# Both parts of h as one moving operand of 512 columns, in an encoder block on one Trainium2 core

## The chip, the cores and the metric

The kernel runs on one core of a Trainium2 chip. The metric is the device time of one execution in microseconds (us), from the first to the last instruction with the little that lies around them. Five engines work at the same time and wait for each other through semaphores: PE (TensorE: matmuls, with weight loads shown apart as PEld), DVE (VectorE), ACT (ScalarE), POOL (GpSimd) and SP (SyncE, which issues most transfers).

## The reference, cut to what matters

`x` is 256 tokens by 2048 channels. One wide projection of the normalised input feeds everything else:

```python
h = rms_norm(x, g_pre)
proj = h @ w_in                      # 256 x 2048 @ 2048 x 10688
mla_in, rwkv_in, z_mla, z_rwkv, gate_mla, gate_rwkv = split(proj)
# attention branch (8 heads) from mla_in; bidirectional recurrent branch (RWKV-7, 16 heads) from rwkv_in
u_mla  = (y_mla  * silu(z_mla))  @ w_br_mla
u_rwkv = (y_rwkv * silu(z_rwkv)) @ w_br_rwkv
out = (sigmoid(gate_mla) * u_mla + sigmoid(gate_rwkv) * u_rwkv) @ w_out
x + rms_norm(out, g_post)
```

## The kernel before

**Two parts.** To keep precision, every float32 operand of a large matmul is split into two float32r parts, hi and lo, with hi + lo the original. A product is then three matmuls: weights hi with h hi, weights hi with h lo, weights lo with h hi. The input h lies in SBUF as `hhi` and `hlo`, channels on partitions, 256 tokens along the row, 16 blocks of 128 channels (`KT`).

**A projection task** (`in_task`, through `cm_task`) makes 256 columns of `proj` as two pieces of 128 output channels. It loads its weights in four chunks of 512 KB (`raw`, three buffers); ACT casts a chunk to `whi` (line 327) and DVE subtracts to get `wlo` (line 330); each has three buffers. For each of the 16 blocks k and each of the two pieces, PE runs lines 396, 397 and 398, all three with 256 moving columns and into the same half of one PSUM bank. So a task uses one bank: piece 0 in its columns 0 to 255, piece 1 in 256 to 511. When the task is done, its `end` stream takes the sums out of the bank (for example `mix` on line 417, `ev_z` on 520, `low_rank_task` on 545).

**Banks.** Eight PSUM banks are named: `d0` to `d2` (pool `DB`, line 215) for projection tasks, `m0` to `m4` (pool `MB`, line 214) for the small products of the two branches.

**The recurrent branch** is worked off in four quads (`Q` 0 to 3, 256 channels each), one after the other. For a quad, `front_d`, `front_k` and `front_v` make its inputs; `chunks_of` then forms the *grams* (line 797 on PE, with the mask multiply on line 191 taking them out of their banks, and transposes on line 805 copied out on line 784), solves a triangular system by 60 small DVE operations and five DVE transposes (lines 818 to 850: the *solve*), and walks through four steps of a recurrence (lines 892 to 944 on PE, 916 to 927 on ACT and DVE). `head_sums` (line 581) are the matmuls of lines 587 and 588.

**Order.** All engines run their instructions in the order in which they were written. That order is made ahead of time by the class `Streams`: each piece of work is a Python generator that asks for an engine with an assumed cost; the class picks the request that can start first, by its own clock, and of those within a small slot the one of the best rank. An operation of a stream is taken as ready `LAG` after the stream's operation before (0.25 us behind PE, 0.12 us behind ACT or DVE, line 49). Projection matmuls have the last rank, so they fill the time that quads leave on PE. `Free.take` hands out banks and work tiles; a stream that finds none waits in the order-making until one is given back. `W.take(KEEP)` asks that more than 6 work tiles are free.

Of the kernel before, what the change touches and what calls it, by code (L numbers as in the profile page):

```python
# [15 lines left out]
S = 256  # L16
D = 2048
# [26 lines left out]
class Streams:  # L44
# [13 lines left out]
    def add(self, gen, rank, t=0.0):  # L58
        s = [gen, rank, t, None]
        self.live.append(s)  # L60
        self._next(s, None)
        return s
# [15 lines left out]
    def run(self, until=None):  # L78
        while self.live and not (until and until()):
# [29 lines left out]
            e, cost = s[3][0], s[3][1]  # L109
            if e == "P":  # L110
# [31 lines left out]
def cD(n):  # L142
    return 0.08 + 1.04e-3 * n
# [11 lines left out]
def encoder_block_kernel(  # L155
# [52 lines left out]
    hhi, hlo = sb([128, KT, S], "hhi", dt=F32R), sb([128, KT, S], "hlo", dt=F32R)  # L208
# [5 lines left out]
    MB = Free(pps.tile([128, 512], F32, tag=f"m{i}", bufs=1, name=f"m{i}") for i in range(5))  # L214
    DB = Free(pps.tile([128, 512], F32, tag=f"d{i}", bufs=1, name=f"d{i}") for i in range(3))
# [155 lines left out]
    def cm_task(src, nk, xhi, xlo, mt, wd, end, kc=4, load_fn=None, ready=None, kready=None, k_first=0,  # L371
                begin=None, pairs=None, first_alone=False):

        parts = []
        nb = (len(mt) + 1) // 2
# [3 lines left out]
        for i, k0 in enumerate(k0s):  # L379
# [23 lines left out]
        def take():  # L403
            b = []
            for _ in range(nb):
                b.append((yield from DB.take()))
            return b

        add_task(parts, begin or take, end, ready)
# [56 lines left out]
    def ev_second(b):  # L466
        yield ("W", lambda: len(have.get("part", ())) == 2)
        for p, m, t, B in zip(b, (96, 128), have["part"], (DB, MB)):
            yield ("D", cD(512))
            tt(w2d(t)[0:m], w2d(t)[0:m], p2(p)[0:m], ALU.add)  # L470
            B.give(p)
# [48 lines left out]
    def ev_z(b, o):  # L520

        z = p2(b[0])
        t = yield from W.take()
        yield ("A", cA(512), None, "exp")
        act.activation(w2d(t), z, AF.Tanh, scale=0.5)
        yield ("D", cD(512))
        stt(o, w2d(t), 1.0, z, ALU.add, ALU.mult)
        W.give(t)
        DB.give(*b)
# [8 lines left out]
    def gate_mla_task(g):  # L538
        def end(b):
            yield ("A", cA(512), None, "exp")  # L540
            act.activation(m16[:, 2 * g:2 * g + 2], p2(b[0]), AF.Tanh, scale=0.5)
            DB.give(*b)
# [1111 lines left out]
```

## Time and profile before

| | us |
|---|---|
| median of three runs | 875.97 |
| lowest and highest | 873.17, 876.22 |
| profiled execution, whole | 872.72 |
| its span, first to last instruction | 870.9 |

The profile is one further execution, 3.25 us below the median and inside 0.5% of it. In it PE is busy for 97% of the span, DVE for 76%, ACT for 58%. PE's matmuls overlap (each is shown with its own full latency), so that neighbouring starts, not the shown length, tell how long one occupies PE.

### The profile page before, as it was taken

The numbers are of one execution on the slowest core, as the hardware profiler recorded it, in microseconds if no ns is written. First come the engines' busy times: TensorE is split into PE (matmuls) and PEld (weight loads), VectorE is DVE, ScalarE is ACT, GpSimd is POOL, SyncE is SP. The second block draws the span as 40 slices with busy tenths as digits, with TensorE's granted clock in tenths as the row PEclk, the third lists the DMA queues.
The fourth block names the chain that finished last, engine by engine and source line by source line (L and its number), as shares of the span: only waits on it lengthen the run. The fifth ranks groups of instructions, "written<-read, shape, count | busy, mean of one in ns | idle before, by whom it ended". The sixth has DMA issues, their size and how long they took to land.

```text
span 870.9 us, 19398 instructions
## 1 busy us (share of the span) xinstructions
PE 848.3 (97%) x8112; PEld 810.0 (93%) x8112; DVE 659.3 (76%) x1082; ACT 501.1 (58%) x797; POOL 30.7 (4%) x66
## 2 busy tenths in 40 slices
PE   9999999999999999999999999999999999999996
PEld 8999999988899998999889999899999999998884
DVE  5878898868987878988789878775867556775554
ACT  6777644487544578354776445586766434444442
POOL 4110000000000000000000000000000000000000
PEclk9999999999999999999999999999999999999999
DMA  9565646633376523565423665346444675555553
GB/s 286 169 181 148 176 129 187 169 99 90 101 212 177 161 68 97 158 193 169 132 76 96 195 188 152 98 149 186 136 128 147 232 257 190 176 193 193 194 195 119
DMA packets 123528, 139.41 MB, mean 160 GB/s; under 512 B 6704, under 2 KB 110512, under 8 KB 123056
## 3 DMA queue, kind: packets, MB, share of 16 engines
q1 hardware_dynamic: 121664, 135.16, 52.4%
q0 software_dynamic: 768, 1.57, 0.6%
q10 hardware_dynamic: 1008, 1.44, 0.5%
q8 instruction: 63, 1.03, 0.5%
q14 instruction: 25, 0.20, 0.1%
HBM read 136.05 MB, written 2.10 MB: 159 GB/s over the span
## 4 chain that ended last, share of the span: by engine, by line
PE 73%; DVE 14%; ACT 8%; issue 2%; DMA 2%; DVEq 0%; ACTq 0%
PE d L396 16%; PE d L398 16%; PE d L397 15%; DVE wlo L330 4%; PE m L1334 2%; PE m L1335 2%; PE m L1336 2%; ACT whi L327 2%; DVE work L191 2%; PE m L398 2%; PE m L396 2%; PE m L397 2%; PE d L1335 1%; PE d L1334 1%; PE d L1336 1%
## 5 line engine op out<-in xcount | busy, mean ns | idle before, releaser
L327 ACT CAST whi<-raw 128x1024 fp32r<-128x1024 f32 (+3 forms) x252 | 252.8, 1004 | 254.2 <-PE d L397 155.1
L330 DVE TENSOR_TENSOR wlo<-raw,whi 128x1024 fp32r<-128x1024 f32 (+3 forms) x250 | 292.4, 1171 | 125.0 <-ACT whi L327 123.4
L396 PE MATMUL d<-hhi,whi 128*128 128x256 f32 (+1 forms) x1296 | 375.1, 289 | 0.0
L398 PE MATMUL d<-hhi,wlo 128*128 128x256 f32 (+1 forms) x1296 | 366.5, 283 | 2.3 <-DVE wlo L330 2.3
L397 PE MATMUL d<-hlo,whi 128*128 128x256 f32 (+1 forms) x1296 | 366.2, 283 | 0.0
L396 PEld LDWEIGHTS d<-hhi,whi 128*128 128x128 f32 (+1 forms) x1296 | 246.8, 190 | 4.5
L398 PEld LDWEIGHTS d<-hhi,wlo 128*128 128x128 f32 (+1 forms) x1296 | 246.9, 190 | 2.7 <-DVE wlo L330 2.7
L397 PEld LDWEIGHTS d<-hlo,whi 128*128 128x128 f32 (+1 forms) x1296 | 247.1, 191 | 0.1
L191 DVE TENSOR_TENSOR work<-work,work 128x512 f32<-128x512 f32 (+5 forms) x64 | 38.8, 612 | 3.9 <-ACT work L575 1.2
L191 DVE TENSOR_TENSOR u<-u,tmp 128x30 f32<-128x30 f32 (+7 forms) x120 | 29.9, 250 | 3.0
L191 DVE TENSOR_TENSOR tmp<-u 128x30 f32<-128x30 f32 (+7 forms) x120 | 29.8, 249 | 2.9
L396 PE MATMUL d<-b,whi 128*128 128x256 f32 x96 | 27.1, 282 | 0.0
L398 PE MATMUL d<-b,wlo 128*128 128x256 f32 x96 | 27.1, 282 | 0.0
L398 PE MATMUL d<-ar,wlo 128*128 128x256 f32 x96 | 27.0, 281 | 0.0
L397 PE MATMUL d<-work,whi 128*128 128x256 f32 x96 | 26.9, 280 | 0.0
L397 PE MATMUL d<-ar,whi 128*128 128x256 f32 x96 | 26.9, 280 | 0.0
L396 PE MATMUL d<-ar,whi 128*128 128x256 f32 x96 | 26.8, 279 | 0.0
L1334 PE MATMUL m<-whi,hhi 128*128 128x512 f32 x60 | 23.3, 389 | 0.0
L1335 PE MATMUL m<-wlo,hhi 128*128 128x512 f32 x60 | 23.3, 389 | 0.0
L1336 PE MATMUL m<-whi,hlo 128*128 128x512 f32 x60 | 23.3, 389 | 0.0
L191 DVE TENSOR_TENSOR g<-m,mask 128x512 f32<-128x512 f32 x32 | 20.6, 686 | 0.0
L797 PE MATMUL m<-ar,u 64*128 64x128 f32 x256 | 19.2, 285 | 0.3 <-DVE g L191 0.3
(334 smaller groups left out, 1487.3 us busy)
## 6 DMA issues: line engine op xcount, KB each, us to landing
raw<-in_w_in_dram SPq DMA_DIRECT2D x160, 512.0 KB, 3.9
raw<-in_w_out_dram SPq DMA_DIRECT2D x32, 512.0 KB, 3.6
raw<-in_w_br_mla_dram SPq DMA_DIRECT2D x16, 512.0 KB, 4.0
raw<-in_w_br_rwkv_dram SPq DMA_DIRECT2D x16, 512.0 KB, 3.3
raw<-in_mla_wkv_b_dram SPq DMA_DIRECT2D x8, 512.0 KB, 3.9
raw<-in_mla_wq_b_dram SPq DMA_DIRECT2D x8, 384.0 KB, 3.3
raw<-in_w_in_dram SPq DMA_DIRECT2D x7, 384.0 KB, 5.3
g<-in_x_dram SPq DMA_DIRECT2D x2, 1024.0 KB, 6.9
```

The lines of the kernel that those rows point to most:

```text
L191: dve.tensor_tensor(out=o, in0=a, in1=b, op=op)
L327: act.copy(dst(c.hi), src(raw))
L330: eng.tensor_tensor(out=dst(c.lo), in0=src(raw), in1=dst(c.hi).bitcast(F32), op=ALU.subtract)
L396: pe.matmul(o, hi[:, c:c + m], xhi(k), start=k == k_first and i % 2 == 0, stop=False)
L397: pe.matmul(o, hi[:, c:c + m], xlo(k), start=False, stop=False)
L398: pe.matmul(o, lo[:, c:c + m], xhi(k), start=False, stop=last)
L797: pe.matmul(m[:, q * 128:q * 128 + 128], z.kb[R64[h], d, j, q], z.ar[d][R64[h], j, q], start=q == 0, stop=q == 3)
L1334: pe.matmul(banks[t], hhi[:, k, T], hi, start=k == 0, stop=False)
L1335: pe.matmul(banks[t], hhi[:, k, T], lo, start=False, stop=False)
L1336: pe.matmul(banks[t], hlo[:, k, T], hi, start=False, stop=k == KT - 1)
```

## The change

Three edits. First, `hhi` and `hlo` become two halves of one tile `hh`, and a projection task runs, per block and piece, one matmul of 512 moving columns (weights hi with h hi and h lo side by side; line 408 of the changed kernel) and one of 256 (weights lo with h hi, added to the first half; line 409). A piece now fills a bank of its own, so a task takes two banks, and its `end` first calls `total`: two ACT copies of the second halves and two DVE adds of the first halves. This goes for 32 tasks; the eight of `gate_rwkv` and the two low-rank tasks at the start keep three matmuls. Second, the pools become four and four banks. Third, `Streams` drops `LAG` where a stream asks twice in a row for the same engine.

```diff
@@ class Streams: add, run
-        s = [gen, rank, t, None]
+        s = [gen, rank, t, None, ""]
...
                     ready = s[2] if len(q) < 3 or q[2] is None else q[2]
+                    if s[4] == q[0] and ready == s[2]:
+
+                        ready -= self.LAG[q[0]]
...
             e, cost = s[3][0], s[3][1]
+            s[4] = e
@@ tiles and banks
-    hhi, hlo = sb([128, KT, S], "hhi", dt=F32R), sb([128, KT, S], "hlo", dt=F32R)
+    hh = sb([128, 2, KT, S], "hh", dt=F32R)
+    hhi, hlo = hh[:, 0], hh[:, 1]
...
-    MB = Free(pps.tile([128, 512], F32, tag=f"m{i}", bufs=1, name=f"m{i}") for i in range(5))
-    DB = Free(pps.tile([128, 512], F32, tag=f"d{i}", bufs=1, name=f"d{i}") for i in range(3))
+    MB = Free(pps.tile([128, 512], F32, tag=f"m{i}", bufs=1, name=f"m{i}") for i in range(4))
+    DB = Free(pps.tile([128, 512], F32, tag=f"d{i}", bufs=1, name=f"d{i}") for i in range(4))
@@ cm_task
+                        if both:
+
+                            o = p2(banks[i])[0:m]
+                            pe.matmul(o, hi[:, c:c + m], both(k), start=k == k_first, stop=False)
+                            pe.matmul(o[:, 0], lo[:, c:c + m], xhi(k), start=False, stop=k == nk - 1)
+                            continue
...
-                steps.append((len(mt) * 3 * 0.119, mm) + (((lambda k=k: kready(k)),) if kready else ()))
+                steps.append((len(mt) * (0.347 if both else 3 * 0.119), mm) + (((lambda k=k: kready(k)),) if kready else ()))
...
-        add_task(parts, begin or take, end, ready)
+        add_task(parts, lambda: take_banks(len(mt) if both else (len(mt) + 1) // 2), end, ready)
@@ in_task and the ends
+        kw.setdefault("both", lambda k: hh[:, :, k])
...
+    def total(b, o):
+
+        for i in range(2):
+            yield ("A", cA(256) - 0.05)
+            act.copy(o[:, i], p2(b[i])[:, 1])
+        for i in range(2):
+            yield ("D", cD(256))
+            tt(o[:, i], p2(b[i])[:, 0], o[:, i], ALU.add)
+            DB.give(b[i])
...
                 t = yield from W.take(KEEP)
-                yield from mix(p2(b[0]), 128, V_MU + 8 * n + 2 * Q, w2d(t))
-                DB.give(*b)
+                yield from total(b, w2d(t))
+                yield from mix(w2d(t), 128, V_MU + 8 * n + 2 * Q, w2d(t))
...
             t = yield from W.take(KEEP)
-            yield ("A", cA(512))
-            act.copy(w2d(t), p2(b[0]))
-            DB.give(*b)
+            yield from total(b, w2d(t))
```

`ev_z` and `gate_mla_task` get `total` in the same way. The order that comes out differs on every engine; three places show how. A name such as `d0_110` is bank `d0` with a serial number.

On PE, a projection task inside a transition between two quads, before: two times three matmuls for block k, pieces 0 and 1, all into bank `d0`.

```order
L396 MATMUL d0_110<-hhi_13_75,whi1_19_81 128x256
L397 MATMUL d0_110<-hlo_14_76,whi1_19_81 128x256
L398 MATMUL d0_110<-hhi_13_75,wlo1_22_84 128x256
L396 MATMUL d0_110<-hhi_13_75,whi1_19_81 128x256
L397 MATMUL d0_110<-hlo_14_76,whi1_19_81 128x256
L398 MATMUL d0_110<-hhi_13_75,wlo1_22_84 128x256
```

And the start of a task in the changed kernel: two matmuls each into `d0` and `d1`, then the next block.

```order
L408 MATMUL d0_108<-hh_13_75,whi1_18_80 128x512
L409 MATMUL d0_108<-hh_13_75,wlo1_21_83 128x256
L408 MATMUL d1_109<-hh_13_75,whi1_18_80 128x512
L409 MATMUL d1_109<-hh_13_75,wlo1_21_83 128x256
L408 MATMUL d0_108<-hh_13_75,whi1_18_80 128x512
L409 MATMUL d0_108<-hh_13_75,wlo1_21_83 128x256
```

What moved: a piece has one matmul fewer, of twice the columns, and a bank of its own.

On PE, the last rows ahead of the grams of quad 3, and the first of these, before (the tile `u8` holds the quad's inputs; between the matmuls of lines 587 and 588 some rows earlier and the grams stand projection matmuls, first into `d0`, then, the task being done, into `d1`):

```order
L398 MATMUL d0_110<-hhi_13_75,wlo0_21_83 128x256
L396 MATMUL d0_110<-hhi_13_75,whi0_18_80 128x256
L397 MATMUL d0_110<-hlo_14_76,whi0_18_80 128x256
L398 MATMUL d0_110<-hhi_13_75,wlo0_21_83 128x256
L396 MATMUL d1_111<-hhi_13_75,whi1_19_81 128x256
L397 MATMUL d1_111<-hlo_14_76,whi1_19_81 128x256
L398 MATMUL d1_111<-hhi_13_75,wlo1_22_84 128x256
L396 MATMUL d1_111<-hhi_13_75,whi1_19_81 128x256
L397 MATMUL d1_111<-hlo_14_76,whi1_19_81 128x256
L398 MATMUL d1_111<-hhi_13_75,wlo1_22_84 128x256
L797 MATMUL m3_108<-ar_182_5302,u8_179_5261 128x128
L797 MATMUL m1_106<-ar_182_5302,u8_179_5261 128x128
```

The same place in the changed kernel, from the last projection matmuls ahead of the grams to the first grams (line 817 is 797 of before, 668 is 648, 607 and 608 are 587 and 588):

```order
L408 MATMUL d2_110<-hh_13_75,whi0_17_79 128x512
L409 MATMUL d2_110<-hh_13_75,wlo0_20_82 128x256
L408 MATMUL d3_111<-hh_13_75,whi0_17_79 128x512
L409 MATMUL d3_111<-hh_13_75,wlo0_20_82 128x256
L668 MATMUL m1_105<-iv_4_66,work7_154_3535 128x128 x2
L668 MATMUL m1_105<-iv_4_66,work17_169_4330 128x128 x2
L607 MATMUL m2_106<-work5_191_4697,bdr_6_68 128x256
L608 MATMUL m2_106<-work8_192_4698,bdr_6_68 128x256
L607 MATMUL m2_106<-work5_191_4697,bdr_6_68 128x256
L608 MATMUL m2_106<-work8_192_4698,bdr_6_68 128x256
L817 MATMUL m3_107<-ar_181_4586,u8_180_4558 128x128
L817 MATMUL m0_104<-ar_181_4586,u8_180_4558 128x128
```

What moved: between line 944 (964 in the changed kernel) and the first gram there were 26 groups of three projection matmuls, and there are now 6 groups of two; the task on `d2` and `d3` ends here, and the next one begins only behind the last gram's transposes, on `d0`.

On DVE, around the same grams, before: the mask multiplies into `g16`, with splits (line 330) and the quad's output work between them.

```order
L191 TENSOR_TENSOR g16_198_5523<-m4_109,mask_1_63 128x512
L191 TENSOR_TENSOR g16_198_5523<-m2_107,mask_1_63 128x512
L194 SCALAR_TENSOR_TENSOR yr_43_113<-yr_43_113,iv_4_66,work12_190_5428 128x256
L330 TENSOR_TENSOR wlo1_22_84<-raw1_16_78,whi1_19_81 128x1024
L191 TENSOR_TENSOR yr_43_113<-yr_43_113,work15_196_5489 128x512
L191 TENSOR_TENSOR g16_198_5523<-m1_106,mask_1_63 128x512
L191 TENSOR_TENSOR g16_198_5523<-m0_105,mask_1_63 128x512
L194 SCALAR_TENSOR_TENSOR yr_43_113<-yr_43_113,iv_4_66,work2_26_88 128x256 x2
```

The same place in the changed kernel: the last four mask multiplies, then the two adds of `total` that set `d0` and `d1` free, then the first split after 22 rows without one.

```order
L195 TENSOR_TENSOR g16_197_4726<-m3_107,mask_1_63 128x512
L195 TENSOR_TENSOR g16_197_4726<-m0_104,mask_1_63 128x512
L195 TENSOR_TENSOR g16_197_4726<-m1_105,mask_1_63 128x512
L195 TENSOR_TENSOR g16_197_4726<-m2_106,mask_1_63 128x512
L195 TENSOR_TENSOR work8_195_4710<-d0_108,work8_195_4710 128x256
L195 TENSOR_TENSOR work8_195_4710<-d1_109,work8_195_4710 128x256
L342 TENSOR_TENSOR wlo0_20_82<-raw0_14_76,whi0_17_79 128x1024
L198 SCALAR_TENSOR_TENSOR yr_42_112<-yr_42_112,iv_4_66,work2_189_4681 128x256 x2
L195 TENSOR_TENSOR yr_42_112<-yr_42_112,work5_194_4709 128x512
```

What moved: the eight mask multiplies stand together, no split is between them, and the banks for the next task come free behind them.

## Rows read from the trace of the kernel before

**Rows 1.** Page: busy time of each engine, share of the span, instructions.

```profile
PE 848.3 (97%) x8112; PEld 810.0 (93%) x8112; DVE 659.3 (76%) x1082; ACT 501.1 (58%) x797; POOL 30.7 (4%) x66
```

**Rows 2.** Busy time by stretch: PE, PEld, DVE, ACT, POOL, granted clock, DMA.

```profile
100.00:560.00 460.00, 449.86 (x5166) 431.43 (x5165) 390.17 (x677) 266.62 (x412) 13.11 (x31) 1.00 0.51 142
```

**Rows 3.** Waits of PE: us in total, times, longest.

```profile
PE m L923 <- DVE work L918: 3.1, 8, 0.7
PE d L398 <- DVE wlo L330: 2.3, 2, 1.2
PE m L587 <- ACT work L435: 1.3, 2, 0.7
```

**Rows 4.** Timeline of PE in a projection task: start, length, instruction.

```profile
682.07 0.28 PE L396 MATMUL d<-hhi,whi 128*128 128x256 f32 x1
...
682.43 0.28 PE L396 MATMUL d<-hhi,whi 128*128 128x256 f32 x1
```

**Rows 5.** Timeline of PE in the output projection, 512 moving columns.

```profile
780.06 0.39 PE L1334 MATMUL d<-whi,hhi 128*128 128x512 f32 x1
...
780.74 0.39 PE L1334 MATMUL d<-whi,hhi 128*128 128x512 f32 x1
```

**Rows 6.** Groups of PE by line: count, busy us, mean ns, idle before.

```profile
L396 PE MATMUL d<-hhi,whi 128*128 128x256 f32 (+1 forms) x1296 | 375.1, 289 | 0.0
...
L396 PE MATMUL m<-hhi,whi 128*128 128x256 f32 x48 | 13.7, 286 | 0.0
```

**Rows 7.** Timeline of PE, a moving operand in two pieces of 128 columns.

```profile
578.19 0.28 PE L1086 MATMUL d<-whi,b 128*128 128x256 f32 x1
578.31 0.28 PE L1087 MATMUL d<-wlo,b 128*128 128x256 f32 x1
```

**Rows 8.** Groups of DVE and ACT that read 256 or 512 columns of PSUM.

```profile
L191 DVE TENSOR_TENSOR work<-m,work 128x256 f32<-128x256 f32 x8 | 3.4, 422 | 3.9 <-PE m L1212 3.9
...
L1205 ACT COPY work<-m 128x256 f32<-128x256 f32 x16 | 5.8, 377 | 1.8 <-PE m L1203 1.8
...
L549 ACT COPY work<-d 128x512 f32<-128x512 f32 x4 | 2.3, 578 | 0.0
```

**Rows 9.** Busy by stretch: quad 0's solve; quad 3's front end; quad 3's grams.

```profile
113.40:173.00 59.60, 59.60 (x498) 59.51 (x497) 51.13 (x95) 27.58 (x32) 0.12 (x1) 1.00 0.59 163
...
448.20:460.50 12.30, 12.27 (x113) 11.85 (x112) 10.83 (x15) 12.15 (x21) 0.52 (x1) 1.00 0.38 103
460.50:472.40 11.90, 11.90 (x124) 11.01 (x124) 11.71 (x20) 7.88 (x13) 0.00 (x0) 1.00 0.27 84
```

**Rows 10.** DVE in quad 0's solve: its one large wait, and the splits.

```profile
DVE wlo L330 <- ACT whi L327: 6.4, 13, 0.7
...
L330 DVE TENSOR_TENSOR wlo<-raw,whi 128x1024 fp32r<-128x1024 f32 x20 | 24.5, 1225 | 6.5 <-ACT whi L327 6.4
```

**Rows 11.** Timeline of ACT ahead of quad 3's grams.

```profile
448.22 1.05 ACT L327 CAST whi<-raw 128x1024 fp32r<-128x1024 f32 x1 [0.33 <-PE d L397]
...
458.96 1.28 ACT L573 ACT_TABLE_LOAD   x1
...
460.80 0.57 ACT L549 COPY work<-d 128x512 f32<-128x512 f32 x1
```

**Rows 12.** Timeline of PE there: recurrence's end, first gram, transposes, second gram.

```profile
448.23 0.69 PE L944 MATMUL m<-g,uv 128*64 128x64 f32 x16
...
460.49 1.16 PE L797 MATMUL m<-ar,u 64*128 64x128 f32 x16
461.58 0.39 PE L396 MATMUL d<-hhi,whi 128*128 128x256 f32 x1
...
462.40 0.60 PE L805 MATMUL m<-iv,u 128*128 128x128 f32 x4
462.76 0.36 PE L396 MATMUL d<-hhi,whi 128*128 128x256 f32 x1
```

**Rows 13.** Timeline of DVE: two grams taken out of their banks.

```profile
461.88 1.28 DVE L191 TENSOR_TENSOR g<-m,mask 128x512 f32<-128x512 f32 x2
```

More of the change, by code (lines that the diff above doesn't have):

```diff
@@ L213, in encoder_block_kernel, with take_banks @@
     W = Free(works[:-1])
-    MB = Free(pps.tile([128, 512], F32, tag=f"m{i}", bufs=1, name=f"m{i}") for i in range(5))
-    DB = Free(pps.tile([128, 512], F32, tag=f"d{i}", bufs=1, name=f"d{i}") for i in range(3))
+    MB = Free(pps.tile([128, 512], F32, tag=f"m{i}", bufs=1, name=f"m{i}") for i in range(4))
+    DB = Free(pps.tile([128, 512], F32, tag=f"d{i}", bufs=1, name=f"d{i}") for i in range(4))
+    def take_banks(n):
+        b = []
+        for _ in range(n):
+            b.append((yield from DB.take()))
+        return b
     yr = sb([128, 8, 256], "yr")
@@ L371, in cm_task @@
     def cm_task(src, nk, xhi, xlo, mt, wd, end, kc=4, load_fn=None, ready=None, kready=None, k_first=0,
-                begin=None, pairs=None, first_alone=False):
+                pairs=None, first_alone=False, both=None):
         parts = []
-        nb = (len(mt) + 1) // 2
         k0s = list(range(k_first, nk, kc))
@@ L467, in ev_second @@
         yield ("W", lambda: len(have.get("part", ())) == 2)
-        for p, m, t, B in zip(b, (96, 128), have["part"], (DB, MB)):
+        for p, m, t in zip(b, (96, 128), have["part"]):
             yield ("D", cD(512))
             tt(w2d(t)[0:m], w2d(t)[0:m], p2(p)[0:m], ALU.add)
-            B.give(p)
+            DB.give(p)
         yield from ev_wd(have["part"][0])
@@ L520, in ev_z @@
     def ev_z(b, o):
-        z = p2(b[0])
+        yield from total(b, o)
         t = yield from W.take()
         yield ("A", cA(512), None, "exp")
-        act.activation(w2d(t), z, AF.Tanh, scale=0.5)
+        act.activation(w2d(t), o, AF.Tanh, scale=0.5)
         yield ("D", cD(512))
-        stt(o, w2d(t), 1.0, z, ALU.add, ALU.mult)
+        stt(o, w2d(t), 1.0, o, ALU.add, ALU.mult)
         W.give(t)
-        DB.give(*b)
     def z_task(c0, key):
@@ L539, in end @@
         def end(b):
+            o = m16[:, 2 * g:2 * g + 2]
+            yield from total(b, o)
             yield ("A", cA(512), None, "exp")
-            act.activation(m16[:, 2 * g:2 * g + 2], p2(b[0]), AF.Tanh, scale=0.5)
-            DB.give(*b)
+            act.activation(o, o, AF.Tanh, scale=0.5)
         in_task(GM0 + 256 * g, end)
@@ L547, in end @@
             t = yield from W.take(KEEP)
-            yield ("A", cA(512))
-            act.copy(w2d(t), p2(b[0]))
-            DB.give(*b)
+            yield from total(b, w2d(t))
             have[key] = t
@@ L1047, in begin @@
             if g == 0:
-                yield ("W", lambda: quads[3].done and len(MB.tiles) > 1)
-                DB.give(MB.tiles.pop())
+                yield ("W", lambda: quads[3].done)
                 att["kT"] = sb([128, 2, 8, 256], "g16", dt=F32R)
@@ L1061, in begin @@
                     tt(t[R64[i]], kr[R64[i]], att["kr"][0][R64[i]].bitcast(F32), ALU.subtract)
-            a = yield from DB.take()
-            b = yield from DB.take()
-            return a, b
+            return (yield from take_banks(2))
         parts = []
@@ L1104, in wq_task @@
         wq_v = wq_b.rearrange("(k p) (h c) -> p k h c", p=128, c=192)
-        def begin():
-            a = yield from DB.take()
-            b = yield from DB.take()
-            return a, b
         parts = []
@@ L1156, in end @@
                 O.add(head(g, i), 1, O.free["D"])
-        add_task(parts, begin, end, lambda: have["qhl"][1] if "qhl" in have else None)
+        add_task(parts, lambda: take_banks(2), end, lambda: have["qhl"][1] if "qhl" in have else None)
     def half_split(src, hi, lo, n):
@@ L1273, in end @@
             th2[g] = t
-        in_task(GR0 + 256 * g, end)
+        in_task(GR0 + 256 * g, end, both=None)
     def split_y():
@@ L1319, in begin @@
                 MB.tiles.clear()
-            a = yield from DB.take()
-            b = yield from DB.take()
-            return a, b
+            return (yield from take_banks(2))
         parts, more = [], []
@@ L1356, in gain @@
             tt(fin["og"][:, t, N], b[t], fin["gpb"][:, N], ALU.mult)
-            DB.give(b[t])
         def end(b):
@@ L1362, in end @@
                 yield from gain(b, t)
+                DB.give(b[t])
             fin["left"] -= 2
@@ L1523, in pairs_first @@
                ("kr", 0 if k0 < 2 else 2 if k0 < 8 else 8))
-    def begin_second():
-        a = yield from DB.take()
-        b = yield from MB.take()
-        return a, b
     LORA = [(0, 96), (128, 96), (256, 128), (384, 128)]
@@ L1532, in encoder_block_kernel @@
     cm_task(None, KT, *HX, LORA, 512, ev_second, kc=2, pairs=pairs_first, load_fn=load_first, kready=lambda k: have.get(("h", k)),
-            k_first=UN, begin=begin_second)
+            k_first=UN)
     rwkv_tasks(0, kready=lambda k: have.get(("h", k)))
```

5 lines of the change are left out of this document (removed).

## The prediction, made before the change was run

> **What bounds the kernel now.** The share of busy time comes first: PE 97% of the span, DVE 76%, ACT 58% [rows 1]. PE's matmuls overlap in the profile, so 97% alone doesn't show that PE is full; the stretches and the waits do. From 100 to 560 us, where the projection tasks fill what the four quads leave, PE is busy for 449.9 of 460 us at a granted clock of 1.00, and DVE for 390.2, which is 85% [rows 2]. Among PE's waits none is above 3.1 us in total [rows 3]: the recurrence's copies (3.1), a split that came late (2.3), the head sums (1.3). So time is won by giving PE less to do, and lost wherever something makes PE wait that now doesn't. DVE, at 85%, is the engine to watch.
>
> **The change, part by part.** *PE's work.* Four neighbouring starts of 256 columns lie 0.36 us apart, 0.120 us for one [rows 4]; three steps of 512 columns take 0.68 us, 0.227 for one [rows 5]. A block and piece costs 3 x 0.120 = 0.360 us before and 0.227 + 0.120 = 0.347 after, 0.013 less. The groups of line 396 count 1296 + 48 = 1344 [rows 6]; the code takes from them 64 of the two low-rank tasks and 256 of the eight `gate_rwkv` tasks, which keep three matmuls. That leaves 1024, and 1024 x 0.013 = 13.3 us. The new moving operand lies in two pieces far apart; line 1086 already moves two pieces of 128 columns and its next start follows after 0.12 us as well [rows 7], so I charge nothing for that.
>
> Here the Trainium skill speaks against the change. By "TensorE: Matmul & The Clock Gate", section "Back-to-back issue gap", a warm matmul costs its columns at 2.4 GHz plus 2.5 ns, so joining two would save 2.5 ns, 2.6 us in all. The rows differ: 256 and 512 columns differ by 107 ns, which is 256 columns at 2.4 GHz, and leave 13 ns fixed in both. The measurement decides; the sum goes on with 13.3.
>
> *The evictions.* Each of 32 tasks gains two ACT copies and two DVE adds of 256 columns out of PSUM. The nearest rows read 0.377 and 0.422 us [rows 8]: 24 us of ACT, less 4 x 0.58 for the low-rank copies that fall away, and 27 us of DVE. Two independent DVE operations overlap by 0.08 us (two grams take 1.28 us, not 2 x 0.68 [rows 13]), so an add holds DVE for 0.34. Neither engine sets the end by itself; what they cost is what PE comes to wait for.
>
> *The solves.* In quad 0's solve PE is full for all of 59.6 us, while DVE works 51.1 [rows 9] and waits 6.4 us, in front of the splits, for ACT's casts [rows 10]; these in turn wait for PE to free a buffer. That wait is the cover. About 20 chunks pass [rows 10]; each is now 8 x 0.013 = 0.10 us shorter on PE, 2.1 in all, and five tasks bring ten adds, 3.4 us. 6.4 - 2.1 - 3.4 = 0.9 us stay, so PE should hardly wait: I take +1 us for the four solves, between 0 and 3.
>
> *The way into quad 3.* This is the largest term against the change. Before, from the recurrence's end (448.23) to the first gram (460.49) is 12.3 us [rows 12], of which ACT is busy for 12.15 [rows 9]: ACT's chain of casts, copies and a table load [rows 11] sets that length, and PE hides it with 26 groups of projection matmuls, 9.4 us. In the changed order 6 groups stand there, 2.1 us, beside 0.7 us of `front_d`'s matmuls that stood ahead of it before; 6.6 us of cover are gone. The reason is in the banks: a low-rank task's `end` waits for a work tile (its copy, line 549, came late before as well, at 460.80 [rows 11]) and holds `d0` and `d1`; before, PE went on in the third bank, now two tasks hold all four. ACT's list there has lost three casts (3.1 us) and gained the second half of `front_d` (about as much), so I keep the 12 us: PE waits 6, between 3 and 9. Behind the grams the next task waits for two mask multiplies and the adds: +1.
>
> *The grams.* Before, projection matmuls stand between the gram matmuls (460.49 to 461.58) and the transposes (462.40 to 462.76) and behind these [rows 12]. DVE empties the two gram banks from 461.88 to 463.16 [rows 13]. In the changed order nine of twelve following groups stand with little or nothing between, and with four `m` banks instead of five the second group needs a bank of the first: PE could begin it 1.6 us after the first one's start, the first bank comes free after 2.1, the other after 2.7. I take 0.5 us each, +4.5 in all; 0 if the spare bank covers it, 9 if DVE has other work first.
>
> *Relief.* In the recurrences one to four k-steps of projection now stand where one or two stood in front of line 923, and same-engine work of a stream runs on without a gap. PE waits there 3.1 us, for the head sums 1.3, and smaller ones [rows 3]; I take -3, between 0 and -6. What follows the last quad, and the start, keep their work: nothing.
>
> **The sum.** -13.3 + 1 + 6 + 1 + 4.5 - 3 = -3.8 us against the profiled execution of 872.72, that is 868.9. The median of the runs lies 3.25 above that execution: 872.2, given as 872. All bounds to one side give -15 or +9.
>
> **The rivals.** *The waits stay hidden.* The dropped `LAG` lets the quads' chains run closer, so banks and operands come early; the gram bank that is spare covers the rest. For it: ACT's three casts fewer on the way into quad 3. Against it: the 6.6 us of cover are gone in any case. The whole change is then -13.3 with at most 5 back, less a little relief: 862 to 868.5.
>
> *The waits take it all.* The way into quad 3 at its upper bound (9) and the grams at 6 to 9: -1 to +4, 875.5 to 880.4.
>
> *Slower: DVE sets the solves.* If the adds don't overlap (0.42 instead of 0.34) and one dependent operation more waits per chunk, the 0.9 us left become a lack; each solve then lasts as long as DVE's list, and 2.5 us in each of four give +10 upon the sum. It decides from the point at which DVE's own work in the stretch exceeds PE's 57.5 us. For it: DVE's 85%. Against it: 6.4 us of measured slack. 880.4 to 888.
>
> *The joined matmul saves almost nothing.* If in this stream a 512-column matmul with a 256-column one behind it took 0.237 us and not 0.227, the saving would be 3 us instead of 13.3 and the sum 10 us worse, 882. Both spacings of the trace speak against that [rows 4, 5]. The page named above would have it so.
>
> **How the numbers follow.** As worked out (868.5 to 875.5) 0.45; hidden 0.25; all taken 0.14; DVE the bound 0.14; no saving 0.02. What a measurement of this kernel tells from no change is about 0.5%, 4.4 us: below 871.6 it is faster, above 880.4 slower. Of the first case about 0.19 lies below 871.6. Faster: 0.25 + 0.19 = 0.44; same: 0.26 + 0.14 = 0.40; slower: 0.14 + 0.02 = 0.16. The range leaves out a sliver of the hidden case and the upper half of the slower ones: 863 to 882. The likeliest case's own is 868.5 to 875.5.
>
> **What the changed profile would show.** PE's term: starts 0.227 and 0.120 us apart inside a task. Solves: PE full, DVE's wait for casts near 1 us instead of 6.4. Way into quad 3: a PE idle of some 6 us ahead of the first gram, ended by DVE's `ar`, with a long run of DVE rows without a split. Grams: PE waits of about half a microsecond ended by DVE `g` or ACT `b`. I would be wrong in the main step if that idle is absent, and in the solves if waits of line 409 for `wlo` add up to more than 3 us.

## The result: 1.2% slower, outside the range

The changed kernel takes 884.89 us, the median of 4 runs (883.29 to 887.56), beside 874.57 us (872.94 to 876.22) for the kernel before in the same job. The ratio is 1.0118, 95% interval 1.0087 to 1.0149. Forecast were 872 us and a range of 863 to 882. Of the runs below, one execution of 1631.8 us (LAG for DVE and ACT) is disturbed and left out of its median.

The profile shows an execution of 887.56 us, with a span of 885.8; before it was 872.72. So the two profiled executions lie 14.8 us apart and the medians 10.3. Line numbers are those of the changed kernel: 408 is the joined matmul, 409 the one with the low part of the weights, 433 the added copy, 817 the grams, 825 their transposes, 943 the recurrence's matmul (797, 805 and 923 before). First the page's busy times (as [rows 1]) and the granted clock in 40 slices:

```profile
PE 851.0 (96%) x7088; PEld 757.0 (85%) x7088; DVE 682.3 (77%) x1146; ACT 519.1 (59%) x857; POOL 30.9 (3%) x66
...
PEclk9999999999999999999996999999999999999998
```

1024 matmuls fewer, 64 DVE and 60 ACT instructions more, as costed. New is the 6 in the row of the clock. Next come busy times by stretch: the stretch of [rows 2], quad 0's solve (as [rows 9]), and the time around quad 3's grams in pieces of 4 us, with the granted clock behind POOL's column:

```profile
100.00:560.00 460.00, 441.51 (x4061) 377.41 (x4060) 403.05 (x720) 277.15 (x454) 12.91 (x30) 0.98 0.50 140
...
115.00:173.00 58.00, 58.00 (x330) 50.31 (x329) 54.28 (x106) 30.07 (x41) 0.12 (x1) 1.00 0.63 175
...
456.00:460.00 4.00, 1.50 (x11) 0.93 (x10) 1.91 (x3) 3.56 (x8) 0.00 (x0) 1.00 0.09 30
460.00:464.00 4.00, 1.65 (x20) 1.27 (x20) 3.52 (x6) 3.91 (x6) 0.00 (x0) 1.00 0.00 0
464.00:468.00 4.00, 3.34 (x20) 2.85 (x20) 3.03 (x6) 1.18 (x3) 0.00 (x0) 0.61 0.00 0
468.00:472.00 4.00, 3.33 (x22) 2.50 (x20) 1.09 (x3) 1.66 (x4) 0.00 (x0) 0.50 0.02 4
472.00:476.00 4.00, 3.31 (x21) 2.50 (x20) 1.49 (x3) 1.53 (x2) 0.00 (x0) 0.50 0.00 0
476.00:480.00 4.00, 3.28 (x10) 2.80 (x11) 3.61 (x7) 0.59 (x1) 0.00 (x0) 0.50 0.18 18
480.00:484.00 4.00, 4.00 (x20) 3.47 (x19) 0.62 (x2) 1.60 (x3) 0.00 (x0) 0.76 0.32 113
```

PE stands idle 18.5 of the 460 us, before it was 10.1. In the solve PE is full and DVE nearly so. Around quad 3's grams PE works 1.50 and 1.65 us of 4 and then runs at a granted clock of 0.50, the 1.2 GHz level; summed over the last five rows it is there for 17 us, and PE is busy for about 15 of these. PE's waits, as [rows 3]:

```profile
PE m L817 <- ACT uv L673: 3.0, 1, 3.0
PE m L943 <- DVE work L938: 2.9, 6, 0.8
PE m L817 <- DVE g L195: 2.7, 5, 1.0
PE d L409 <- DVE wlo L342: 2.2, 3, 1.3
PE m L607 <- ACT work L457: 2.2, 1, 2.2
...
PE m L817 <- ACT b L804: 1.4, 2, 0.7
```

All rows of this view add up to 25.5 us in 46 waits; before, to 13.8 us in 31. The timeline of PE at quad 3's grams, as [rows 12]:

```profile
458.61 0.38 PE L607 MATMUL m<-work,bdr 128*128 128x256 f32 x1 [2.16 <-ACT work L457]
...
459.89 1.16 PE L817 MATMUL m<-ar,u 64*128 64x128 f32 x16
460.99 0.66 PE L825 MATMUL m<-iv,u 128*128 128x128 f32 x4
464.66 2.68 PE L817 MATMUL m<-ar,u 64*128 64x128 f32 x16 [3.01 <-ACT uv L673]
467.27 1.11 PE L825 MATMUL m<-iv,u 128*128 128x128 f32 x4
469.06 2.08 PE L817 MATMUL m<-ar,u 64*128 64x128 f32 x16 [0.68 <-ACT b L804]
...
476.72 0.80 PE L408 MATMUL d<-hh,whi 128*128 128x512 f32 x1 [0.73 <-DVE work L195]
```

No projection matmul stands between 456 and 476.72. The same sixteen gram matmuls take 1.16 us at the first group and 2.08 at the third: the clock.

### The profile page after: what moved, and what is told of

Its sections match the earlier page's. It is cut to its first block, busy times and chain, and to the rows that moved or that the text cites. A ratio compares the mean times of both kernels' runs of the same rounds, so it can differ in the third digit from the quotient of the medians.

```text
span 885.8 us, 17493 instructions
## 1 busy us (share of the span) xinstructions
PE 851.0 (96%) x7088; PEld 757.0 (85%) x7088; DVE 682.3 (77%) x1146; ACT 519.1 (59%) x857; POOL 30.9 (3%) x66
## 4 chain that ended last, share of the span: by engine, by line
PE 67%; DVE 18%; ACT 10%; issue 4%; DMA 2%; SPq 0%; DVEq 0%; ACTq 0%
PE d L408 18%; PE d L409 9%; PE d L413 6%; PE d L415 6%; PE d L414 6%; DVE wlo L342 5%; DVE work L195 2%; PE m L1344 2%; PE m L1345 2%; PE m L1346 2%; PE d L1345 2%; PE d L1344 2%; PE d L1346 2%; ACT whi L339 2%; DVE work L198 2%
## 5 line engine op out<-in xcount | busy, mean ns | idle before, releaser
L408 PE MATMUL d<-hh,whi 128*128 128x512 f32 x1024 | 370.1, 404 | 0.7 <-DVE work L195 0.7
L409 PE MATMUL d<-hh,wlo 128*128 128x256 f32 x1024 | 288.3, 282 | 2.2 <-DVE wlo L342 2.2
L408 PEld LDWEIGHTS d<-hh,whi 128*128 128x128 f32 x1024 | 193.5, 189 | 47.6 <-DVE work L195 1.1
L409 PEld LDWEIGHTS d<-hh,wlo 128*128 128x128 f32 x1024 | 194.5, 190 | 3.1 <-DVE wlo L342 3.1
L413 PE MATMUL d<-hh,whi 128*128 128x256 f32 (+1 forms) x320 | 93.0, 291 | 0.0
L414 PE MATMUL d<-hh,whi 128*128 128x256 f32 (+1 forms) x320 | 90.3, 282 | 0.6 <-DVE hh L198 0.6
L415 PE MATMUL d<-hh,wlo 128*128 128x256 f32 (+1 forms) x320 | 90.3, 282 | 0.1
L414 PEld LDWEIGHTS d<-hh,whi 128*128 128x128 f32 (+1 forms) x320 | 60.2, 188 | 0.9 <-DVE hh L198 0.9
L413 PEld LDWEIGHTS d<-hh,whi 128*128 128x128 f32 (+1 forms) x320 | 60.1, 188 | 0.9
L415 PEld LDWEIGHTS d<-hh,wlo 128*128 128x128 f32 (+1 forms) x320 | 60.2, 188 | 0.4 <-DVE wlo L342 0.4
L413 PE MATMUL d<-b,whi 128*128 128x256 f32 x128 | 36.1, 282 | 0.0
L414 PE MATMUL d<-ar,whi 128*128 128x256 f32 x128 | 35.9, 280 | 0.0
L413 PE MATMUL d<-ar,whi 128*128 128x256 f32 x128 | 35.7, 279 | 0.0
```

The source lines that it names most:

```text
L408: pe.matmul(o, hi[:, c:c + m], both(k), start=k == k_first, stop=False)
L409: pe.matmul(o[:, 0], lo[:, c:c + m], xhi(k), start=False, stop=k == nk - 1)
L413: pe.matmul(o, hi[:, c:c + m], xhi(k), start=k == k_first and i % 2 == 0, stop=False)
L414: pe.matmul(o, hi[:, c:c + m], xlo(k), start=False, stop=False)
L415: pe.matmul(o, lo[:, c:c + m], xhi(k), start=False, stop=last)
```

## The experiments

All ratios are to the kernel before, timed in the same job; its median was 873.5 to 874.0 us there. Times are medians.

### What joining saves

*Three matmuls in the changed order*: 890.7 us, 1.0185 (1.0171 to 1.0199).

```diff
-    pe.matmul(o, hi[:, c:c + m], both(k), start=k == k_first, stop=False)
+    pe.matmul(o[:, 0], hi[:, c:c + m], xhi(k), start=k == k_first, stop=False)
+    pe.matmul(o[:, 1], hi[:, c:c + m], xlo(k), start=False, stop=False)
```

> The changed kernel in exactly its own order, but each joined matmul of 512 columns is issued as two of 256 into the two halves of the same bank; banks, adds, copies and planner costs are unchanged. The difference to the changed kernel is what joining alone saves. By the prediction (0.013 us each, 1024 times) this is 13.3 us slower than the changed kernel, 898. By the starts in the changed kernel's trace (0.2355 + 0.1175 instead of 0.360) it is 7 us slower, 892. By the gap that the Trainium skill's page TensorE: Matmul & The Clock Gate gives, 2.6 us, 887.5.

*h side by side*: 886.1 us, 1.0138 (1.0124 to 1.0152).

```diff
-    hh = sb([128, 2, KT, S], "hh", dt=F32R)
+    hh = sb([128, KT, 2, S], "hh", dt=F32R)
```

> The changed kernel in exactly its own order, but the two parts of h lie side by side for each k-step, so that the moving operand is one piece of 512 columns instead of two pieces of 256 that lie 16 KB apart. Theory A (the two pieces cost the 9 ns by which the joined matmul's start is later than 0.227): starts fall from 0.236 to 0.227 and the time by up to 9 us, 876 to 879. Theory B (the 9 ns come from the shorter matmul or the weight load beside it, or from writing the bank): starts stay at 0.236 and the time at 885.

Undoing the join alone costs 5.8 us against the changed kernel's own runs and 4.6 against the run with h side by side, which was timed in the same job: 5 to 6 us, give or take 2 to 3 us by the intervals, and not 13.3. The timelines of PE inside a task of the changed kernel and, below, of the one with h side by side show why:

```profile
130.68 0.40 PE L408 MATMUL d<-hh,whi 128*128 128x512 f32 x1
130.91 0.28 PE L409 MATMUL d<-hh,wlo 128*128 128x256 f32 x1
131.03 0.40 PE L408 MATMUL d<-hh,whi 128*128 128x512 f32 x1
131.26 0.28 PE L409 MATMUL d<-hh,wlo 128*128 128x256 f32 x1
```

```profile
129.15 0.40 PE L408 MATMUL d<-hh,whi 128*128 128x512 f32 x1
129.39 0.28 PE L409 MATMUL d<-hh,wlo 128*128 128x256 f32 x1
129.50 0.40 PE L408 MATMUL d<-hh,whi 128*128 128x512 f32 x1
```

The start behind a joined matmul comes after 0.236 us and the next after 0.117 (the medians of about 1000 such pairs), 0.353 in all instead of 0.347. By the starts alone joining would save 1024 x 0.007, some 7 us. The spacing is the same with the operand in one piece, so the two pieces are free, as the prediction had it; a 512-column matmul with a 256-column one behind it is slower by 9 ns than in the stream of nothing but 512 [rows 5]. Why, no run isolates.

### The way into quad 3, and the clock

*Low-rank tasks wait for 3 spare work tiles instead of 6*: 884.5 us, 1.0121 (1.0107 to 1.0134).

```diff
@@ low_rank_task
-            t = yield from W.take(KEEP)
+            t = yield from W.take(3)
```

> The changed kernel with one number changed: the low-rank tasks wait until more than 3 work tiles are free instead of more than 6. The order is the changed kernel's up to the third quad's grams; after that 25.6 us of projection matmuls stand between the recurrence's end and the first gram of quad 3 instead of 2.1. Theory A (the lost cover ahead of quad 3, and the granted clock that falls behind it, make most of the loss): no idle of over 1 us in front of quad 3's first gram, granted clock 1.00 in every 25 us window between 425 and 525, and 10 to 13 us less than the changed kernel, 872 to 875. Theory B (the added adds and copies make the chains late wherever cover stands, the idle only moves): quad 3 begins earlier but the time stays between 881 and 887. If only the idle counts and the clock costs nothing: 5 us less, about 880.

Theory B's time came: the idle at the grams is gone, the loss is not. (Its other part did not come: quad 3's first gram starts at 488.4 us, later than the changed kernel's 459.9.) On the way into quad 3 the timeline of PE has a longer pause instead, which ends with the DVE add that frees a `d` bank, and behind it the matmul's length doubles. (A second pause, of 3.2 us, stands at 583 us in front of the head sums, line 607.) The first:

```profile
468.43 0.40 PE L408 MATMUL d<-hh,whi 128*128 128x512 f32 x1
468.66 0.28 PE L409 MATMUL d<-hh,wlo 128*128 128x256 f32 x1
472.72 0.79 PE L408 MATMUL d<-hh,whi 128*128 128x512 f32 x1 [3.78 <-DVE work L195]
```

*One pause in the kernel before*, by repeating one cast of a weight chunk in quad 1's solve: with six casts more 878.3 us, 1.0048 (1.0034 to 1.0062); with nine 881.5 us, 1.0083 (1.0068 to 1.0098).

```diff
                 act.copy(dst(c.hi), src(raw))
+                for _ in range(6 if i == 76 else 0):
+                    act.copy(dst(c.hi), src(raw))
```

> The kernel before in its own order; in the middle of quad 1's solve, where PE has nothing but projection matmuls, one cast of a weight chunk on ACT is made seven times instead of once (6 x 1.03 us more). PE then pauses once, by about 3 us: 6.2 us less some 3 us that the splits run ahead. Theory A (the granted clock falls behind a pause of this length and takes its own time): a window with a clock near 0.50 behind the pause and a time longer by clearly more than the pause, 6 us or more in all. Idle only: as long as the pause, +3 us, no window below 1.00.

> As the kernel with six casts more, with nine (9.3 us more on ACT): PE pauses by about 6 us. Theory A: 6 us of pause and the same fall of the clock behind it, so 3 us longer than the kernel with six. Idle only: +6 us upon the kernel before.

Busy times by stretch of 4 us around the pause, first with six casts, then with nine:

```profile
276.00:280.00 4.00, 2.96 (x25) 2.76 (x23) 0.00 (x0) 3.87 (x5) 0.00 (x0) 1.00 0.00 0
280.00:284.00 4.00, 2.55 (x11) 2.35 (x12) 3.19 (x7) 2.54 (x3) 0.00 (x0) 0.74 0.20 35
284.00:288.00 4.00, 4.00 (x31) 4.00 (x30) 3.76 (x12) 1.55 (x2) 0.00 (x0) 0.84 0.79 231
```

```profile
276.00:280.00 4.00, 0.98 (x9) 0.78 (x7) 0.00 (x0) 3.87 (x5) 0.00 (x0) 1.00 0.00 0
280.00:284.00 4.00, 1.60 (x5) 1.31 (x6) 1.98 (x5) 3.75 (x4) 0.00 (x0) 0.54 0.00 0
284.00:288.00 4.00, 4.00 (x23) 4.00 (x23) 3.83 (x10) 0.27 (x1) 0.00 (x0) 0.61 0.77 184
```

PE is idle for 2.5 us with six casts (1.04 and 1.45 of the first two rows) and for 5.4 with nine; both times the clock falls, and the kernel loses 4.4 and 7.6 us, about 2 more than the pause each time. By the intervals the losses are at least 3.0 and 5.9 us, which is still above the pauses. So the fall of the clock has a price of its own, as theory A had it. The first pause was expected at 3 us and the loss at 6 or more; the size was off, the mechanism held.

### LAG and the banks

*The changed kernel without the LAG edit*: 913.3 us, 1.0450 (1.0435 to 1.0464).

```diff
-                        ready -= self.LAG[q[0]]
+                        ready -= 0.0
```

> The changed kernel without the planner's LAG edit: a stream's next operation on the same engine is again given its delay. Joined matmuls, four and four banks, adds and copies stay. 2.8 to 3.6 us of projection matmuls stand again between the gram groups of the first three quads, and 1.4 us ahead of quad 3. Theory A (the shortage of banks ahead of quad 3 makes the loss, the LAG edit little): idle ahead of quad 3's grams of 5 us or more and a granted clock below 0.95 again in a window behind it, time 880 to 887. Theory C (the LAG edit makes the loss, by taking the cover between grams away): PE waits at the grams fall by 4 us or more in all and the time is 872 to 878.

*LAG alone in the kernel before* (the planner's edited lines, nothing else; cut here): 880.1 us, 1.0077 (1.0065 to 1.0090).

```diff
+                    if s[4] == q[0] and ready == s[2]:
+                        ready -= self.LAG[q[0]]
```

> The kernel before with the planner's LAG edit alone: three matmuls, five and three banks, one eviction. In its order 10 to 22 us of projection matmuls stand ahead of the grams of quads 1 to 3, almost none between the gram groups. Theory C (running a stream's operations on without the delay shortens the quads' chains in any kernel, and in the changed kernel it hid a loss of nearly 30 us): faster than before, 860 to 868, with the solves as long as before and less idle of PE than 68.7 us. Theory D (it pays only where the added evictions have made the chains late): within 4 us of before, 870 to 878. By the term of the prediction (relief 3 us, grams 4.5 us): 875.

*LAG, four `m` and four `d` banks*, three matmuls and one bank a task: 884.4 us, 1.0123 (1.0106 to 1.0140). *LAG and two `d` banks*: 896.9 us, 1.0268 (1.0248 to 1.0288). *Two `d` banks without LAG*: 891.0 us, 1.0198 (1.0183 to 1.0212).

```diff
-    MB = Free(pps.tile([128, 512], F32, tag=f"m{i}", bufs=1, name=f"m{i}") for i in range(5))
-    DB = Free(pps.tile([128, 512], F32, tag=f"d{i}", bufs=1, name=f"d{i}") for i in range(3))
+    MB = Free(pps.tile([128, 512], F32, tag=f"m{i}", bufs=1, name=f"m{i}") for i in range(4))
+    DB = Free(pps.tile([128, 512], F32, tag=f"d{i}", bufs=1, name=f"d{i}") for i in range(4))
```

> The kernel before with the LAG edit and four m and four d banks, as in the changed kernel, so four tasks in flight and one m bank less. Theory H (the m bank that was taken away makes PE wait in the grams and the solves): 4 us or more slower than the LAG edit alone, with the added waits at the gram matmuls. Otherwise within 3 us of it.

> The kernel before with the LAG edit and two d banks instead of three: one bank for each task, so two tasks in flight as in the changed kernel, without joined matmuls and adds. Theory G (the shortage of banks is the loss): 6 us or more slower than the LAG edit alone, and PE waits of over 1 us ended by the eviction of a d bank. Theory F: within 3 us of it.

> The kernel before with two d banks instead of three, so two tasks in flight, without the LAG edit. Cover at the grams and ahead of the quads as before (8.6 to 10.8 us). Theory G (two tasks in flight are too few whatever the order): 8 us or more slower than before, with PE waits of over 2 us for an eviction. Theory A: they matter only where the cover runs out: within 4 us of before up to the last quad, and a few us behind it, where each task takes two banks; 876 to 882.

(With two `d` banks the 3 becomes a 2, and nothing else.) The expectations of LAG fell, both of each pair: it costs the kernel before 6 us, and in the changed kernel it saves 28. (Without it the changed kernel's profile has 44.7 us of PE waits instead of 25.5, and the clock is at the lower level for some 58 us between 485 and 619 us.) Theory H's number came (4.3 us more than LAG alone), but its reason did not: PE's waits at the grams are 2.9 us with four and four banks and 3.8 with LAG alone. G's number came too: two `d` banks cost 17 us with and without LAG. But without LAG none of that lies in the quads, which run as before: the first gram comes 7.1 us later (at 108.7 instead of 101.6), and what follows the last recurrence takes 11.4 us longer (319.0 instead of 307.6). PE's waits name the tasks behind quad 3, which need two banks each, and the start (line 396). With two `d` banks such a task is alone in flight; in the changed kernel, with four, it is not, so at least the 11.4 us are no price that the changed kernel pays.

```profile
PE d L1086 <- DVE g L191: 5.1, 2, 2.8
PE d L396 <- DVE work L191: 3.6, 1, 3.6
```

### The evictions

*The evictions' work in the kernel before*, in front of each task's old eviction, the planner not told: 893.6 us, 1.0226 (1.0212 to 1.0240). *The planner told*: 900.9 us, 1.0312 (1.0295 to 1.0330). (Cut; the comments give the second run's costs.)

```diff
+        for i in range(2):
+            yield ("A", -0.12)            # told: cA(256) - 0.05
+            act.copy(o[:, i], p2(b[0])[:, i])
+        for i in range(2):
+            yield ("D", -0.12)            # told: cD(256)
+            tt(o[:, i], p2(b[0])[:, i], o[:, i], ALU.add)
```

> The kernel before (three matmuls, five and three banks, no LAG edit) with the work of the changed kernel's evictions added to each of the 32 tasks: two ACT copies and two DVE adds of 256 columns out of the bank, into the task's own destination, which the old eviction then overwrites. The planner is not told of them, so its order stays that of before but for small moves. Theory F (the added 27 us of DVE and 20 us of ACT delay what PE waits for): 6 us or more slower than before, with waits for splits or evictions. By the prediction's term for the solves (1 us, between 0 and 3) and little elsewhere: 874 to 878.

> The same with the planner told of the copies and adds at the costs that the changed kernel gives them, so that it makes its order with them, without joined matmuls, without the LAG edit, with five and three banks. Theory I (the planner's order with the added operations, not the operations themselves, makes PE idle; the changed kernel without the LAG edit lost 39 us that way): 15 us or more slower than before. Theory F: as slow as with the planner not told, within 4 us.

Theory F's loss came in the first run, though only 2.0 us of PE's waits there are for a split. In the second theory I's 15 us or more came, and F's "within 4 us" did not: the planner's own order adds 7 us. In nearly the order of before, the copies and adds alone cost 20 us; they also hold each bank longer, and the run doesn't part the two. PE's waits in that kernel (lines 936 and 925 are the recurrence's matmuls, 875 the small ones behind the solve, 810 the grams, 398 the third projection matmul), two of its stretches of 20 us, and below them one of the kernel before:

```profile
PE m L936 <- DVE work L931: 5.2, 7, 1.1
PE m L875 <- DVE u L880: 2.7, 7, 1.4
PE m L925 <- DVE z L191: 2.5, 4, 0.8
PE m L810 <- DVE g L191: 2.1, 3, 1.6
PE d L398 <- DVE wlo L330: 2.0, 2, 1.8
```

```profile
360.00:380.00 20.00, 19.67 (x154) 19.35 (x155) 19.40 (x33) 9.44 (x13) 1.01 (x2) 0.91 0.46 133
480.00:500.00 20.00, 18.13 (x142) 17.22 (x143) 17.89 (x26) 10.47 (x16) 0.00 (x0) 0.91 0.32 96
```

```profile
480.00:500.00 20.00, 20.00 (x167) 20.00 (x168) 16.68 (x38) 8.64 (x10) 0.00 (x0) 1.00 0.73 211
```

The view adds up to 24.1 us in 43 waits, 10.3 more than before, nearly all on DVE, and no wait is above 1.8 us. Five stretches of 20 us read a clock of 0.91, where before none but the last was below 1.00; each is some 3.6 us at the lower level, so up to 1.8 us of work, 9 us in all. 10 and up to 9 would make nearly all of the 20; that is a sum of readings and not a test.

*The changed kernel without its adds* (the product of the weights' high part with the low part of h is left out of the result): 883.5 us, 1.0110 (1.0097 to 1.0123).

```diff
         for i in range(2):
             yield ("A", cA(256) - 0.05)
-            act.copy(o[:, i], p2(b[i])[:, 1])
-        for i in range(2):
-            yield ("D", cD(256))
-            tt(o[:, i], p2(b[i])[:, 0], o[:, i], ALU.add)
+            act.copy(o[:, i], p2(b[i])[:, 0])
             DB.give(b[i])
```

> The changed kernel without the 64 DVE adds: the two ACT copies stay (now of the first half of each bank) and free the banks, the product with the low part of h is left out of the result. Theory F (the 27 us of adds on a DVE that is already full, and the banks that wait for them, make the idle of PE): DVE falls from 94% to under 90% of the solves, no idle above 2 us and no clock below 1.00 between 440 and 600, time 862 to 870. Theory G (two tasks in flight instead of three, by the banks, make it): the idle ahead of quad 3 or behind it stays, time 878 to 885.

Without the adds the planner makes another order, and in that one PE waits 5.1 us at 459 us for a copy that frees a bank. Theory G's time came (878 to 885), F's 862 to 870 did not, but the order differs from the changed kernel's. So this run doesn't show that the adds are cheap, nor the run before it that they cost 20 us in every order.

### LAG on some engines, and splits on GpSimd

*The changed kernel with LAG for DVE alone*: 876.5 us, 1.0034 (1.0020 to 1.0047). *For DVE and ACT* (`"DA"` in place of `"D"`): 877.4 us, 1.0044 (1.0027 to 1.0060). *The kernel before with LAG for DVE alone*: 877.4 us, 1.0045 (1.0027 to 1.0064).

```diff
-                    if s[4] == q[0] and ready == s[2]:
+                    if s[4] == q[0] in "D" and ready == s[2]:
```

> The changed kernel with the LAG edit limited to DVE: only an operation that follows one of the same stream on DVE is taken without the delay; on PE and ACT the delay stays. Joined matmuls, banks, adds and copies as in the changed kernel. In its order 2.8 to 4.3 us of projection matmuls stand in the grams of all four quads and 10 to 11.4 us ahead of quads 1 to 3 (2.1 ahead of quad 3 in the changed kernel). Theory A (what the changed kernel loses is cover at the grams and ahead of quad 3, and the clock behind it): no idle above 2 us and no window below a clock of 0.98 between 440 and 600, PE idle below 78 us, time 870 to 876. Theory G (two tasks in flight are too few whatever the order): idle of 3 us or more ended by an eviction of a d bank somewhere between 400 and 620, time 880 or more.

> The changed kernel with the LAG edit for DVE and ACT, not for PE. 3.6 to 4.3 us of projection matmuls in the grams of quads 0 to 2 and 0.7 in quad 3's, 5.0 us ahead of quad 3. Theory A: between the changed kernel and the edit for DVE alone, 876 to 882, with an idle of 3 us or more around quad 3's grams and a clock below 0.95 behind it.

> The kernel before with the LAG edit limited to DVE. Grams keep 3.6 to 4.3 us of projection matmuls as in the kernel before, and 11.5 to 13.7 us stand ahead of quads 1 to 3. Theory A: the 6 us that the whole LAG edit costs the kernel before come from the cover it takes out of the grams, so they are gone, 868 to 875. Other (they come from the order of the late tasks): 878 to 882.

As theory A has it, with projection matmuls back in the grams and ahead of quad 3 the changed kernel gets 7 to 8 us back (by the ratios and by the times; the expected 870 to 876 is missed by half a microsecond). For the kernel before neither expectation came: 877.4 lies between 875 and 878. The page of the changed kernel with LAG for DVE alone shows what came back:

```profile
PE 840.5 (96%) x7088; PEld 751.7 (86%) x7088; DVE 681.4 (78%) x1146; ACT 517.0 (59%) x857; POOL 30.8 (4%) x66
```

Its span is 872.9 us, 12.9 less than the changed kernel's. PE's waits fell only from 25.5 to 23.2 us, but PE is busy for 10.5 us less with as many matmuls, and until the last microseconds of the kernel the clock is at the lower level for 3.4 us instead of 17. At half speed 13.7 us less of that are worth up to 6.8 us. The largest of the waits that are left stand at the recurrence (5.3 us in 11) and at the splits:

```profile
PE m L943 <- DVE work L938: 5.3, 11, 1.0
PE d L409 <- DVE wlo L342: 5.0, 3, 2.0
```

*Every fourth split of chunks 30 to 170 on GpSimd* (the planner is told 2.7 us for each), upon that kernel: 919.8 us, 1.0512 (1.0487 to 1.0537). *In the kernel before*: 888.4 us, 1.0163 (1.0141 to 1.0184).

```diff
-WLG = [2, 4]
+WLG = [2, 4] + list(range(30, 170, 4))
```

> The changed kernel with the LAG edit for DVE alone, and every fourth weight split from chunk 30 to 170 on GpSimd instead of DVE (35 splits, 1.22 us each on DVE, so 43 us less DVE work there). Theory F (in the solves the added adds fill DVE, and PE comes to wait for splits: 5.0 us in three waits with the LAG edit for DVE alone): these waits go, and the time falls by 4 us or more, to 868 to 873. If DVE's load is no matter: 874 to 880.

> The kernel before with the same 35 splits on GpSimd, nothing else changed: what the relief of DVE does where no adds were put on it. Theory F: nothing that can be measured, 872 to 876, since PE waits there only 2.3 us for a split.

Both got much slower, against every expectation, so these two don't answer the question on DVE's load. The groups of DVE, first with the change, then in the kernel before, show other DVE operations longer (686 ns and 482 ns without these splits):

```profile
L195 DVE TENSOR_TENSOR work<-work,work 128x512 f32<-128x512 f32 x26 | 21.4, 823 | 10.4 <-ACT work L595 6.4 <-ACT work L733 3.0 <-ACT work L1029 0.9
```

```profile
L194 DVE SCALAR_TENSOR_TENSOR work<-work,iv,work 128x256 f32<-128x256 f32 x16 | 12.7, 821 | 0.1
```

## Why the prediction was wrong

Against the profiled execution the forecast was 868.9 us and the result 887.56, 18.7 more; by the medians it was 872.2 against 884.89, 12.7 more. Two terms account for most of it. The terms of the clock and the waits are read from the one pair of profiled executions; together with the first they come near the 18.7 and are too large for the 12.7, so none of them is sure to a few us.

**PE's work: mis-sized.** 13.3 us were taken, 5 to 6 are there, 7.5 to 8 less. The 0.227 came from a stream of 512-column matmuls only, and the joined one has a 256-column one behind it. The rival with 0.237 us had the spacing nearly right (0.236) and got 0.02. The estimate of 2.6 us from the Trainium skill ("TensorE: Matmul & The Clock Gate", "Back-to-back issue gap", where the 2.5 ns are given for an isolated matmul) lies below the measurement; the rows of before lay above it.

**The clock: not in the sum at all.** The prediction read that it stood at 1.00 from 100 to 560 us [rows 2] and took it as given. But no wait of PE in that kernel was above 1.2 us. The prediction forecast a pause of 6 us and charged 6. PE is busy for about 15 of the 17 us at the lower level, so its work there lasted some 7.5 us longer than at full clock, an estimate from the rows. That a pause costs more than itself is shown by the two kernels with one pause, and the kernel with LAG for DVE alone, which has little of the lower level, wins back 7 to 8 us; the clock's part of the changed kernel's time was not measured by itself.

**The waits: near in sum, by luck, and in other places.** The terms +1, +6, +1, +4.5 and -3 make 9.5 us; PE's waits grew by 25.5 - 13.8 = 11.7. *Solves:* right; PE stands idle 1.9 us in the four, before 2.3, and line 409 waits for `wlo` 2.2 us in all, under the 3 that were to prove it wrong. *Way into quad 3:* near in size (6.2 us against 7), wrong in place and releaser: only 2.5 us stand ahead of the first gram, where 3 to 9 were forecast, 3.0 behind it and 0.7 behind the last gram; ACT ends the two long ones (line 607 for 2.2 us, line 817 for 3.0) and not DVE's `ar`. *Grams:* waits of line 817 for `g` and `b` make 4.1 us against 4.5. *Relief:* did not come; line 943 waits 2.9 us against 3.1, and LAG alone costs the kernel before 6 us. *The start and what follows the last quad*, put at nothing, have some 2 us more: line 1475 (1465 before) waits 2.1 us at the start, before 1.5, and line 1215 waits 1.7 us behind the last quad, before 0.2.

7.5, 7.5 and 2.2 make 17.2 of the 18.7.

**The evictions: looked for in one place.** The step "Neither sets the end by itself; what they cost is what PE comes to wait for" looked for that cost in the solves, where a slack of 6.4 us could be read. The run that adds them alone shows 20 us, half of it in waits of at most 1.8 us each, at the recurrence, behind the solve, at the grams and at a split, and most of the rest, as far as the rows tell, in the lower clock behind such waits. Run by run from the kernel before: LAG +6.3, four and four banks +4.3, evictions and two banks a task +6.3, joining -5.8, which makes the +11. But a ladder in another sequence has other steps: evictions first, told to the planner, +27; LAG last, -28. They are effects of orders, not prices of operations.

**The rivals.** The measured time lies in the interval of "DVE sets the solves" (880.4 to 888), but by luck, since PE is all but full there. The 882 of "The joined matmul saves almost nothing" lies 3 us from the result: its spacing was nearly right, but it too left the clock out.

**What stays open.** Why LAG lengthens the kernel before: taking it back on PE and ACT, which returns the cover to the grams, gives back 2.7 of the 6.3 us; the rest was not tracked down. How far the adds alone cost the changed kernel is open too. No version found beats the kernel before; the best with joined matmuls is 0.34% slower.

## What to carry to other kernels

Before trading PE work for work on engines that feed PE, add that work alone to the old order and time it: here the trade gave 5 to 6 us of PE and cost up to 20, by the order in which it was tried. Read a saving off a pair of instructions that stand in the mixture that the new kernel will have, not in a pure stream. And when a forecast leaves PE idle for some microseconds in a kernel whose granted clock reads 1.00 throughout, add the clock's price to that of the pause: here about 2 us for one pause of 2.5 us.

## What the runs showed of the hardware

A pause of PE of 2.5 us, after more than 30 us in which it was full, was followed by a granted clock near 0.50 for some 3 us although work was there at once (the kernel with six casts more); with 5.4 us of pause it was some 7. In the kernel with the evictions' work, planner not told, waits of 1.0 to 1.8 us stood ahead of four of the five falls; in the kernel before, waits of up to 1.2 us left the clock at 1.00.

With splits on GpSimd (2.5 us each) DVE operations that read two operands in SBUF took longer in the mean: 823 ns instead of 686 for 128x512, 821 instead of 482 for one of 128x256. The Trainium skill has it so ("SBUF — State Buffer", "Who interferes with whom": a DVE instruction with two inputs in SBUF contends with a GpSimd instruction that reads SBUF). The rows agree: the mask multiplies of 128x512, with one operand in PSUM, kept their length in the kernel before (680 ns instead of 686). That kernel lost 14.5 us with these splits; how much of it the longer DVE operations make, and how much the longer splits themselves (1.2 us on DVE), no run isolates.
